# Recurrence scores: the second half's tokens kept in a turned order, and one product for two chunks at six levels

## The chip, the cores and the metric

The kernel runs on one core of one Trainium2 chip. A core has five engines that work side by side and are kept in step by semaphores: TensorE (PE in the profile; its weight loads are shown apart as PEld), VectorE (DVE), ScalarE (ACT), GpSimd (POOL) and SyncE (SP), which mostly issues DMAs. The metric is the device time of one execution in microseconds. Before the change it is 1434.34 us, the median of three runs (1434.25 to 1435.36).

## The reference

The reference is one block of a streaming encoder on 1024 tokens of 1024 channels in float32: a normalisation, a stick-breaking attention and a gated linear recurrence (HGRN2) side by side, a merge with per-channel gates, an output projection, an MLP with squared ReLU, and a last normalisation. The change is in the recurrence. For each of four heads with 128 channels:

```python
f = lb + (1.0 - lb) * sigmoid(f_raw);  k = (1.0 - lb) * sigmoid(-f_raw);  q = silu(q_hg)
# S_t = diag(f_t) S_{t-1} + k_t v_t^T,   o_t = S_t^T q_t, done by chunks:
bcum  = cumsum(log f)                                    # inside a chunk
decay = exp(bcum[t] - bcum[s])  where t >= s, else 0     # (t, s, d)
scores = einsum('td,sd,tsd->ts', q, k, decay)
o      = scores @ v + (q * exp(bcum)) @ state
state  = exp(b_last)[:, None] * state + (k * exp(b_last - bcum)).T @ v
```

The decay between a key's token s and a query's token t is a product over the tokens between them, one for each channel, so the scores of a chunk are not one product of two matrices.

## The kernel before, in words

The kernel holds the recurrence's data with channels on partitions and the 1024 tokens along the free dimension: for each head three tiles of 128x1024, `pp` (the forget factors f, called `dec`), `k` and `q`. Chunks are 128 tokens, eight of them; chunks 0 to 3 are the first half, 4 to 7 the second. The tile `sc` (128x1024) holds the scores of a head, for each chunk 128 key places on partitions by 128 query places. The tile `v` holds the values with tokens on partitions.

`hg_levels(h)` (line 1027) builds `sc` by levels. At level l the chunk is cut into blocks of 2H tokens, H = 2^l; each block has a left half of H tokens (keys) and a right half (queries). At that point `k` in a left half has been multiplied by the decay up to the half's end, `q` in a right half by the decay from the half's start, so the scores between the two are a plain product. After it the left keys are multiplied by the whole decay of the right half and the right queries by that of the left (lines 1144 and 1145), and the two whole decays by each other (line 1146): that prepares the next level. What each level does to get its scores differs:

- The diagonal and level 0 (H = 1) need no product of matrices: `pairs_of` multiplies keys and queries on VectorE, splits the result in a high and a low part (`hi_lo`: a cast on ScalarE, line 156, and a subtraction on VectorE, line 161), and `sums_of` adds over the channels with two products against a matrix of ones, 512 columns each, of the reduced float32 type that TensorE reads in one go.
- Level 1 (H = 2) does the same with two sets of pairs: four such products.
- Levels 2, 3, 4: `scores_of` (line 1034) makes one 128x128 float32 product per chunk, all keys by all queries, and line 1163 copies what a mask selects into `sc`, one copy on VectorE for each half.
- Levels 5 and 6 (H = 32, 64): 16 products of 32 columns from keys and queries that ScalarE had kept aside (line 1120), and eight of 64 columns; ScalarE then copies them to their partitions in `sc` (line 1170).

`hg_tail(h)` (line 1173) turns the keys onto partitions (`pk`), makes the state products with the values (`pkv`), adds up the states, makes the outputs (`pho`), normalises them and turns them back (`pot`) into `on`.

What sets the order of the work: the program is traced in the order of the code, and a planner places each instruction on its engine by priority and by its own forecast of durations; every engine then works in the order thus fixed, a DMA's issue included. PE's work is in two lanes, `main` (attention, recurrence) and `fill` (long projections). Inside a lane the order is kept; `open_block` lets the fill run at most two main blocks ahead of the last finished one (AHEAD = 2). The main program (lines 2370 to 2387) takes a level of head h and a step of head h-1's tail in turn, and after each advances the fill by a few steps of six 512-column products (FILL). The value projection `i_job` (line 948) is such a fill: for each block of 128 tokens, 24 products into `pji`, then ScalarE copies each head's 128 columns into that head's value tile (line 958). Head 0's tail waits with the state products until this job is done (`st.finish(j_i)`, line 1188).

Tiles of 4 KB a partition come from a pool of 40 (`slot`), those of 2 KB from a pool of ten (`slot_n`), PSUM banks from a pool of eight. A tile's place comes free when its last reader is done.

Of the kernel before, what the change touches and what calls it, by code (L numbers as in the profile page):

```python
# [19 lines left out]
P = 128  # L20
T = 1024
# [18 lines left out]
def kernel(  # L40
# [127 lines left out]
    def mul(out, a, b):  # L168
        return nc.vector.tensor_tensor(out=out, in0=a, in1=b, op=ALU.mult)  # L169

# [747 lines left out]
    def f_epilogue(h):  # L918
        def ep(ps, half):
            pp, k = hg_slot(h, "pp", half), hg_slot(h, "k", half)  # L920
            nc.scalar.activation(k, ps, AF.Sigmoid, scale=-1.0)
            nc.scalar.activation(pp, ps, AF.Sigmoid)
# [21 lines left out]

    u_i = wide_unit("wi", W_IN, C_I, HGW)
    u_i.__class__ = ByParts

    def i_job():
        unit = u_i

        vs = []

        def ep(ps, tb):
            for h in range(NHG):
                if tb == 0:
                    vs.append(slot(f"v{h}"))
                    hg[h, "v"] = vs[h]
                nc.scalar.copy(vs[h][:, tb * P : (tb + 1) * P], ps[:, h * P : (h + 1) * P])
            if tb == NT - 1:
                vs.clear()  # L960

        return st.add([unit], lambda: token_steps("pji", unit, xn, range(NT), ep, n=HGW))

    def silu_epilogue(h, key):
        def ep(ps, half):
            t = hg_slot(h, key, half)
            nc.scalar.activation(t, ps, AF.Sigmoid)
            if h < 2:
                x = slot_n(f"qx{h}_{half}", 512)
                nc.scalar.copy(x, ps)  # L970
                ps = x
            mul(t, ps, t)

        return ep
# [17 lines left out]
    def make_masks():  # L992
        mscr = slot_n("mscr", 4 * P, I32)
        mask_bits = hpool.tile([P, 4 * 512], U8, tag="h", name="masks")
        m_x, m_s, m_gt, m_odd = (mscr[:, i * P : (i + 1) * P] for i in range(4))
# [3 lines left out]
        after(nc.vector.tensor_scalar(out=m_odd, in0=m_s, scalar1=1, scalar2=None, op0=ALU.bitwise_and), bounded[0])  # L999
        nc.vector.tensor_tensor(out=m_x, in0=m_x, in1=m_s, op=ALU.bitwise_xor)  # L1000

        def add_mask(l, m_if):
# [3 lines left out]
            m = mask_bits[:, len(masks) * P : (len(masks) + 1) * P]  # L1006
            made = nc.vector.scalar_tensor_tensor(
                out=m, in0=m_s, scalar=1.0, in1=m_if, op0=ALU.is_equal, op1=ALU.mult
            )
            masks.append(m)  # L1010
            masked[0] = made

        for l in (0, *range(2, 5)):
            add_mask(l, m_gt)

        mul(m_odd, m_odd, m_gt)
        add_mask(1, m_odd)
        nc.vector.tensor_tensor(out=m_odd, in0=m_gt, in1=m_odd, op=ALU.subtract)
        add_mask(1, m_odd)
# [7 lines left out]
    def hg_levels(h):  # L1027
# [6 lines left out]
        def scores_of(name):  # L1034
            open_block("main")
            banks = []
            for half in range(2):
                S = bank(f"{name}_{half}")
                for c in range(4):
                    cs = slice((4 * half + c) * P, (4 * half + c + 1) * P)  # L1040
                    matmul(S[:, c * P : (c + 1) * P], k[:, cs], q[:, cs], start=True, stop=True)
                banks.append(S)
            return banks

        def pairs_of(name, *products):

            his, los = [], []
            for i, (a, b, w) in enumerate(products):
# [3 lines left out]
                x = mul(t.rearrange("p (n c) -> p n c", c=w) if w else t, a, b)  # L1052
# [28 lines left out]

        def diagonal(sums, behind=None):
# [3 lines left out]
        pairs = pairs_of(f"sd{h}", *((k[:, cs], q[:, cs], 0) for _, cs in halves()))  # L1086
# [7 lines left out]
        for l in range(7):  # L1094
            H = 1 << l
            n = T // (2 * H)
            if l <= 2:
                sums = sums_of(pairs)
            if l == 0:
                pairs = pairs_of(  # L1100
                    f"sl{h}_{l}", (blocks_of(k, 1)[:, :, 0, 0], blocks_of(q, 1)[:, :, 1, 0], 0)
# [3 lines left out]
            elif l == 1:  # L1105
                if h == 0:
                    u_i.split(3)
                kv, qv = blocks_of(k, 2)[:, :, 0], blocks_of(q, 2)[:, :, 1]
                pairs = pairs_of(
                    f"sl{h}_{l}",  # L1110
                    *((kv[:, :, i : i + 1].to_broadcast([P, T // 4, 2]), qv, 2) for i in (1, 0)),
                )
                if h == 0:
                    u_i.split(4)
            elif l < 5:
                banks = scores_of(f"sl{h}_{l}")
            elif l == 5:
                kept = tuple(slot_n(f"{n}k{h}", 512) for n in "kq")
                for i, (to, src) in enumerate(zip(kept, (k, q))):
                    nc.scalar.copy(  # L1120
                        to.rearrange("p (n h) -> p n h", h=H), blocks_of(src, H)[:, :, i, :]
                    )
# [1367 lines left out]
```

## Time and profile before

| | |
|---|---|
| median of three runs | 1434.34 us |
| profiled execution, its own time | 1434.48 us |
| its span, first to last instruction | 1432.7 us |
| granted TensorE clock, mean | 0.998 |
| TensorE busy | 1421.8 us, 99% of the span |
| VectorE busy | 1106.8 us, 77% |
| ScalarE busy | 678.9 us, 47% |
| GpSimd busy | 150.5 us, 11% |
| DMA, mean rate | 164 GB/s, 235.64 MB moved |

The recurrence runs from about 325 to 570 us of the span, between attention and the merge. How to read the rows: an engine, the line of the kernel, the operation, the tile written, an arrow and the tiles read, with buffer numbers left out (`sl` for the score banks of all heads and levels, `pji` for all value blocks). A float32 product of TensorE leaves two records for each instruction, one of the reduced type leaves one. Starts of PE records show its pace; their lengths overlap, since products are pipelined. Of a DMA, the time to landing is counted from its issue.

### The profile page before, as it was taken

What the parts mean: (1) busy time and instruction counts of PE and PEld (TensorE: products, weight loads), DVE (VectorE), ACT (ScalarE), POOL (GpSimd) and SP (SyncE); (2) the same over time, 40 slices, a digit from 0 to 9 for tenths busy, and PEclk for the clock granted to TensorE, in tenths of its full rate; (3) what the DMA queues carried; (4) which work ended last, traced back from release to release, by engine and by line L of the source; (5) the groups of instructions that cost most, each with busy time, mean ns of one, the idle gap of its engine ahead of it and who ended that gap; (6) DMA issues with size and microseconds to landing.
All of it is one profiled execution on the core that took longest, in us unless ns stands there. A gap on an engine that the chain in (4) does not pass through costs nothing.

```text
span 1432.7 us, 19220 instructions
## 1 busy us (share of the span) xinstructions
PE 1421.8 (99%) x7056; PEld 1195.2 (83%) x7056; DVE 1106.8 (77%) x1511; ACT 678.9 (47%) x1185; POOL 150.5 (11%) x340
## 2 busy tenths in 40 slices
PE   9999999999999999999999999999999999999998
PEld 8888888888888888888888888888888888888886
DVE  7579889888678898898797898666666758668765
ACT  6366676763233445333344673544444433524343
POOL 3012223210011031000000300000000000000042
PEclk9999999999999999999999999999999999999999
DMA  7024546435025775555476405444446974776825
GB/s 241 25 67 126 116 95 111 85 81 148 0 56 158 231 196 189 157 172 190 131 284 237 177 30 198 150 135 146 150 162 218 345 268 154 263 275 252 279 101 180
DMA packets 162038, 235.64 MB, mean 164 GB/s; under 512 B 26220, under 2 KB 93336, under 8 KB 161944
## 3 DMA queue, kind: packets, MB, share of 16 engines
q1 hardware_dynamic: 145480, 190.37, 39.9%
q0 software_dynamic: 11584, 34.61, 9.8%
q10 hardware_dynamic: 4880, 9.44, 1.9%
q8 instruction: 55, 0.90, 0.3%
q14 instruction: 39, 0.32, 0.1%
HBM read 167.27 MB, written 65.01 MB: 162 GB/s over the span
## 4 chain that ended last, share of the span: by engine, by line
PE 97%; DVE 1%; DMA 1%; ACT 1%; POOL 0%; issue 0%; SPq 0%; ACTq 0%; DVEq 0%
PE pm L128 21%; PE pX L128 9%; PE pW L128 6%; PE pY L128 6%; PE pjqk L128 5%; PE pga L128 4%; PE gX L128 4%; PE gY L128 4%; PE pjf L128 3%; PE pys L128 3%; PE pjq L128 3%; PE pji L128 3%; PE pyh L128 3%; PE pjv L128 3%; PE po L128 3%; PE sl L128 3%
## 5 line engine op out<-in xcount | busy, mean ns | idle before, releaser
L156 ACT CAST whid<-w 128x1024 fp32r<-128x1024 f32 x30 | 31.6, 1054 | 154.5 <-PE pm L128 89.8
L814 DVE TENSOR_TENSOR_SCAN rm<-rm,bits 128x511 f32<-128x511 f32 (+7 forms) x72 | 87.2, 1218 | 18.0 <-ACT rm L792 18.0
L128 PE MATMUL pm<-wlod,sh 128*128 128x512 f32 x240 | 93.5, 390 | 0.0
L128 PE MATMUL pm<-whid,sh 128*128 128x512 f32 x240 | 93.4, 389 | 0.0
L128 PE MATMUL pm<-whid,sl 128*128 128x512 f32 x240 | 93.4, 389 | 0.0
L128 PE MATMUL pm<-tl,sh 128*128 128x512 f32 (+1 forms) x210 | 81.3, 387 | 0.0
L128 PE MATMUL pm<-th,sl 128*128 128x512 f32 (+1 forms) x210 | 81.3, 387 | 0.0
L128 PE MATMUL pm<-th,sh 128*128 128x512 f32 (+1 forms) x210 | 81.3, 387 | 0.0
L161 DVE TENSOR_TENSOR wlod<-w,whid 128x1024 fp32r<-128x1024 f32 x30 | 36.6, 1222 | 53.9 <-ACT whid L156 53.9
L161 DVE TENSOR_TENSOR sl<-sa,sh 128x1024 fp32r<-128x1024 f32 x56 | 68.2, 1218 | 0.3 <-ACT sh L156 0.3
L2124 POOL TENSOR_SCALAR fss<-fss 128x1 f32<-128x1 f32 x8 | 4.5, 560 | 562.0 <-ACT fsc L2119 561.4
L156 ACT CAST wTh<-pw 128x512 fp32r<-128x512 f32 (+2 forms) x96 | 43.9, 487 | 40.9 <-PE pw L131 38.6
L156 ACT CAST sh<-sa 128x1024 fp32r<-128x1024 f32 x56 | 57.2, 1045 | 7.1 <-DMA sa<-ad 7.1
L128 PEld LDWEIGHTS pm<-wlod,sh 128*128 128x128 f32 x240 | 45.1, 188 | 9.7 <-DVE wlod L161 0.4
L128 PEld LDWEIGHTS pm<-whid,sh 128*128 128x128 f32 x240 | 45.1, 188 | 9.5
L128 PEld LDWEIGHTS pm<-whid,sl 128*128 128x128 f32 x240 | 45.0, 188 | 9.2
L161 DVE TENSOR_TENSOR wTl<-pw,wTh 128x512 fp32r<-128x512 f32 (+2 forms) x96 | 49.9, 546 | 3.4 <-ACT wTh L156 3.4
L169 DVE TENSOR_TENSOR bt<-bt,rm 128x511 f32<-128x511 f32 (+7 forms) x72 | 49.0, 685 | 4.4 <-DVE rm L814 0.5
L792 ACT ACTIVATE rm<-z 128x511 f32<-128x511 f32 (+4 forms) x96 | 48.2, 502 | 7.5 <-DMA osb<-osb 2.9
L128 PE MATMUL pX<-sql,t1h 128*128 128x512 f32 x128 | 49.9, 390 | 0.0
L128 PE MATMUL pX<-sqh,t1l 128*128 128x512 f32 x128 | 49.9, 390 | 0.0
L128 PE MATMUL pX<-sqh,t1h 128*128 128x512 f32 x128 | 49.8, 389 | 0.0
(936 smaller groups left out, 4479.3 us busy)
## 6 DMA issues: line engine op xcount, KB each, us to landing
w<-in_w_ff_dram SPq DMA_DIRECT2D x72, 512.0 KB, 6.0
sa<-ad SPq DMA_DIRECT2D x56, 512.0 KB, 7.0
ad<-a SPq DMA_DIRECT2D x32, 256.0 KB, 2.5
ad<-s SPq DMA_DIRECT2D x16, 512.0 KB, 5.5
tw<-in_w_out_dram POOLq DMA_DIRECT2D x24, 256.0 KB, 4.9
pr<-pd SPq DMA_DIRECT2D x10, 512.0 KB, 5.2
x<-in_x_dram SPq DMA_DIRECT2D x8, 512.0 KB, 10.0
xnl<-xnh POOLq DMA_DIRECT2D x8, 512.0 KB, 9.0
```

The lines of the kernel that those rows point to most:

```text
L128: return pe(nc.tensor.matmul(*a, **k))
L156: hi_last[0] = after(in_turn("act", nc.scalar.copy(dst, src)), hi_behind[0])
L161: nc.vector.tensor_tensor(out=dst, in0=src, in1=hi.bitcast(F32), op=ALU.subtract),
L169: return nc.vector.tensor_tensor(out=out, in0=a, in1=b, op=ALU.mult)
L792: nc.scalar.activation(rm[:, s0 + c0 - 1 : s0 + m - 1], z[:, c0:m], AF.Sigmoid, scale=-0.125)
L814: sc = nc.vector.tensor_tensor_scan(out=rr, data0=rr, data1=bits[:, 1024 - nk + a : 1024 - nk + b][:, ::-1], initial=rm[:, b : b + 1] if i ...
L2124: nc.gpsimd.tensor_scalar(out=ssq, in0=ssq, scalar1=1.0 / D, scalar2=EPS, op0=ALU.mult, op1=ALU.add)
```

## The change

The tokens of the second half are kept in another order: inside each block of 32 tokens the 16 pairs stand in reverse, so the place of a token has four bits (those of 2, 4, 8 and 16) flipped and the lowest one kept. At levels 1 to 4 the keys of the second half then stand in right halves and its queries in left halves, the other way round than in the first half. One product now takes chunk c of the first half and chunk c + 4 of the second together: 64 keys and 64 queries from each. For that the keys of both are put into one tile by a copy on ScalarE, where each key's column is also its place in the chunk, and the queries are read where they are, by an access pattern that steps from one half to the other. The two quadrants of the result that belong to one chunk are laid into `sc`; the two that cross chunks are not used. Levels 5 and 6, whose bits are not flipped, are done the same way, with the second half's scores copied across partitions by ScalarE. Level 1 no longer goes through pairs and sums.

The order is brought in where the data arise: the activations and multiplies that write `pp`, `k` and `q` of the second half read PSUM with groups of two backwards, and the tail's last activation turns `on` back. The values, which have tokens on partitions, are turned by a trip through DRAM: two blocks of tokens at a time are stored, and loaded back with rows in the new order, both on ScalarE's DMA queue. For this the value tiles hold two token blocks of all four heads each, where they held one head's eight blocks, and the copy out of PSUM is one for all heads. There are two masks for each level from 1 to 4.

```diff
@@ -167,6 +167,18 @@
 
     def mul(out, a, b):
         return nc.vector.tensor_tensor(out=out, in0=a, in1=b, op=ALU.mult)
+
+    def in_groups(t):
+        return t.rearrange("p (c g r) -> p c g r", g=16, r=2)
+
+    def turned_groups(t):
+        return in_groups(t)[:, :, ::-1, :]
+
+    def of_half(t, half):
+        return turned_groups(t) if half else t
+
+    def as_half(t, half):
+        return in_groups(t) if half else t
...
@@ -918,8 +930,9 @@
     def f_epilogue(h):
         def ep(ps, half):
             pp, k = hg_slot(h, "pp", half), hg_slot(h, "k", half)
-            nc.scalar.activation(k, ps, AF.Sigmoid, scale=-1.0)
-            nc.scalar.activation(pp, ps, AF.Sigmoid)
+            ps = of_half(ps, half)
+            nc.scalar.activation(as_half(k, half), ps, AF.Sigmoid, scale=-1.0)
+            nc.scalar.activation(as_half(pp, half), ps, AF.Sigmoid)
...
@@ -942,31 +955,40 @@
+    val_t, stored = [], []
     u_i = wide_unit("wi", W_IN, C_I, HGW)
     u_i.__class__ = ByParts
 
+    def turn_values():
+        while stored:
+            t, vd = stored.pop()
+            rows = vd.rearrange("(n g r) c -> n g r c", g=16, r=2)[:, ::-1]
+            for r in range(2):
+                nc.scalar.dma_start(t[r::2], rows[:, :, r])
+
     def i_job():
         unit = u_i
 
-        vs = []
-
         def ep(ps, tb):
-            for h in range(NHG):
-                if tb == 0:
-                    vs.append(slot(f"v{h}"))
-                    hg[h, "v"] = vs[h]
-                nc.scalar.copy(vs[h][:, tb * P : (tb + 1) * P], ps[:, h * P : (h + 1) * P])
-            if tb == NT - 1:
-                vs.clear()
+            if tb % 2 == 0:
+                val_t.append(slot(f"v{tb // 2}"))
+            cs = slice(tb % 2 * 512, (tb % 2 + 1) * 512)
+            turn_values()
+            nc.scalar.copy(val_t[-1][:, cs], ps)
+            if tb >= NT // 2 and tb % 2:
+                vd = dram(f"vd{tb}", [P, 1024])
+                nc.scalar.dma_start(vd, val_t[-1])
+                stored.append((val_t[-1], vd))
 
     def silu_epilogue(h, key):
         def ep(ps, half):
             t = hg_slot(h, key, half)
+            ps, t = of_half(ps, half), as_half(t, half)
             nc.scalar.activation(t, ps, AF.Sigmoid)
             if h < 2:
-                x = slot_n(f"qx{h}_{half}", 512)
+                x = as_half(slot_n(f"qx{h}_{half}", 512), half)
                 nc.scalar.copy(x, ps)
                 ps = x
             mul(t, ps, t)
@@ -992,31 +1014,26 @@
...
+            for op in ops or (ALU.mult,):
+                m = mask_bits[:, len(masks) * P : (len(masks) + 1) * P]
+                masked[0] = nc.vector.scalar_tensor_tensor(
+                    out=m, in0=m_s, scalar=1.0, in1=m_if, op0=ALU.is_equal, op1=op
+                )
+                masks.append(m)
+
+        add_mask(0, m_gt)
+        for l in range(1, 5):
+            add_mask(l, m_gt, ALU.mult, ALU.is_gt)
 
@@ -1031,25 +1048,41 @@
         dec, k, q = (hg[h, n] for n in ("pp", "k", "q"))
...
-        def scores_of(name):
+        def crossed(t, side, H, c=None, last=False):
+            n = (512 if c is None else P) // (2 * H)
+            step = 512 if H > 16 else 512 - H if side else 512 + H
+            at = t.offset + (c or 0) * P + (side * H + H - 1 if last else side * H)
+            return bass.AP(
+                tensor=t.tensor,
+                offset=at,
+                ap=[list(t.ap[0]), [step, 2], [2 * H, n], [0 if last else 1, H]],
+            )
+
+        def scores_of(name, H):
+            keys = slot_n(f"k{name}", 512)
+            nc.scalar.copy(
+                keys.rearrange("p (n s h) -> p s n h", s=2, h=H), crossed(k, 0, H)
+            )
             open_block("main")
-            banks = []
-            for half in range(2):
-                S = bank(f"{name}_{half}")
-                for c in range(4):
-                    cs = slice((4 * half + c) * P, (4 * half + c + 1) * P)
-                    matmul(S[:, c * P : (c + 1) * P], k[:, cs], q[:, cs], start=True, stop=True)
-                banks.append(S)
-            return banks
+            S = bank(name)
+            for c in range(4):
+                matmul(
+                    S[:, c * P : (c + 1) * P].rearrange("p (s n h) -> p s n h", s=2, h=H),
+                    keys[:, c * P : (c + 1) * P],
+                    crossed(q, 1, H, c),
+                    start=True,
+                    stop=True,
+                )
+            return S
 
...
@@ -1079,11 +1112,29 @@
                 right, m, S.rearrange("p (c n h) -> p c n h", c=NT, h=H)
             )
 
+        def lay_half(l, S, half):
+            H = 1 << l
+            side = 1 if l > 4 else 1 - half
+            to = sc[:, half * 512 : (half + 1) * 512].rearrange(
+                "p (c n two h) -> p c n two h", c=4, two=2, h=H
+            )[:, :, :, side]
+            src = S.rearrange("p (c s n h) -> p c s n h", c=4, s=2, h=H)[:, :, half]
+            if l < 5:
+                m = blocks_of(masks[2 * l - 1 + half], H)[:, :, side]
+                m = m.unsqueeze(1).to_broadcast([P, 4, P // (2 * H), H])
+                nc.vector.copy_predicated(to, m, src)
+                return
+            for b in range(P // (2 * H)):
+                r = 2 * b * H
+                nc.scalar.copy(
+                    to[r : r + H, :, b], src[r + half * H : r + (half + 1) * H, :, b]
+                )
+
...
@@ -1094,84 +1145,50 @@
         for l in range(7):
             H = 1 << l
             n = T // (2 * H)
-            if l <= 2:
+            if l < 2:
                 sums = sums_of(pairs)
             if l == 0:
                 pairs = pairs_of(
-                    f"sl{h}_{l}", (blocks_of(k, 1)[:, :, 0, 0], blocks_of(q, 1)[:, :, 1, 0], 0)
+                    f"sl{h}_{l}", (blocks_of(k, 1)[:, :, 0, 0], blocks_of(q, 1)[:, :, 1, 0])
                 )
                 if h == 0:
                     u_i.split(2)
-            elif l == 1:
-                if h == 0:
+            else:
+                S = scores_of(f"sl{h}_{l}", H)
+                if h == 0 and l == 1:
                     u_i.split(3)
-                kv, qv = blocks_of(k, 2)[:, :, 0], blocks_of(q, 2)[:, :, 1]
-                pairs = pairs_of(
-                    f"sl{h}_{l}",
-                    *((kv[:, :, i : i + 1].to_broadcast([P, T // 4, 2]), qv, 2) for i in (1, 0)),
-                )
-                if h == 0:
                     u_i.split(4)
-            elif l < 5:
-                banks = scores_of(f"sl{h}_{l}")
-            elif l == 5:
-                kept = tuple(slot_n(f"{n}k{h}", 512) for n in "kq")
-                for i, (to, src) in enumerate(zip(kept, (k, q))):
-                    nc.scalar.copy(
-                        to.rearrange("p (n h) -> p n h", h=H), blocks_of(src, H)[:, :, i, :]
-                    )
-            else:
-                open_block("main")
-                small_S = bank(f"sl{h}_5")
-                for i in range(2 * n):
-                    cs = slice(i * H // 2, (i + 1) * H // 2)
-                    matmul(
-                        small_S[0 : H // 2, cs], kept[0][:, cs], kept[1][:, cs],
-                        start=True, stop=True,
-                    )
-                S = bank(f"sl{h}_{l}")
-                for i in range(n):
-                    s0 = i * 2 * H
-                    matmul(
-                        S[0:H, i * H : (i + 1) * H],
-                        k[:, s0 : s0 + H],
-                        q[:, s0 + H : s0 + 2 * H],
-                        start=True,
-                        stop=True,
-                    )
             kv, qv, dv = (blocks_of(t, H) for t in (k, q, dec))
             left, right = (dv[:, :, i, H - 1 : H] for i in range(2))
-            mul(kv[:, :, 0, :], kv[:, :, 0, :], right.to_broadcast([P, n, H]))
-            mul(qv[:, :, 1, :], qv[:, :, 1, :], left.to_broadcast([P, n, H]))
+            if l == 0 or l > 4:
+                mul(kv[:, :, 0, :], kv[:, :, 0, :], right.to_broadcast([P, n, H]))
+                mul(qv[:, :, 1, :], qv[:, :, 1, :], left.to_broadcast([P, n, H]))
+            else:
+                for i, t in enumerate((k, q)):
+                    part = crossed(t, i, H)
+                    mul(part, part, crossed(dec, 1 - i, H, last=True))
             hg_level[0] = mul(right, right, left)
             if l == 0:
                 if h > 0:
                     diagonal(sums)
                 else:
                     first_sums = sums
-            elif l == 1:
-                if h == 0:
-                    diagonal(first_sums, pairs[3])
-                after(lay(masks[0], sums[0], 1), pairs[4] if h == 0 else None)
-            elif l == 2:
-                for m, S in zip(masks[-2:], sums):
-                    lay(m, S, 2)
-            if l < 2:
-                pass
-            elif l < 5:
-                for half_, cs in halves():
-                    nc.vector.copy_predicated(
-                        chunks(sc[:, cs]), over_chunks(masks[l - 1]), chunks(banks[half_])
-                    )
-            elif l == 6:
-                for G, src in ((H // 2, small_S), (H, S)):
-                    for i, b in enumerate(range(0, P, 2 * G)):
-                        part = src[0:G].rearrange("p (c b t) -> p c b t", c=NT, t=G)[:, :, i, :]
-                        nc.scalar.copy(chunks(sc)[b : b + G, :, b + G : b + 2 * G], part)
+            else:
+                if l == 1:
+                    if h == 0:
+                        diagonal(first_sums)
+                    lay(masks[0], sums[0], 1)
+                for half, _ in halves():
+                    lay_half(l, S, half)
             yield
 
     def hg_tail(h):
-        dec, k, q, v, sc = (hg.pop((h, n)) for n in ("pp", "k", "q", "v", "sc"))
+        dec, k, q, sc = (hg.pop((h, n)) for n in ("pp", "k", "q", "sc"))
+
+        def v(c):
+            at = c % 2 * 512 + h * P
+            return val_t[c // 2][:, at : at + P]
+
         on_t = slot(f"on{h}")
         fc = small.tile([P, NT], F32, tag="fc", name=f"fc{h}")
         nc.vector.tensor_copy(fc, chunks(dec)[:, :, P - 1])
@@ -1186,13 +1203,14 @@
             nc.scalar.copy(ktk[:, half * 512 : half * 512 + n * P], pk[:, : n * P])
         yield
         st.finish(j_i)
+        turn_values()
         open_block("main")
         for half in range(2):
             pkv = bank(f"pkv{h}_{half}")
             for j in range(4 - half):
                 c = 4 * half + j
                 cs, js = slice(c * P, (c + 1) * P), slice(j * P, (j + 1) * P)
-                matmul(pkv[:, js], ktk[:, cs], v[:, cs], start=True, stop=True)
+                matmul(pkv[:, js], ktk[:, cs], v(c), start=True, stop=True)
             for j in range(4 - half):
                 c = 4 * half + j
                 cs, js = slice(c * P, (c + 1) * P), slice(j * P, (j + 1) * P)
@@ -1218,7 +1236,7 @@
             for j in range(4):
                 c = 4 * half + j
                 cs, js = slice(c * P, (c + 1) * P), slice(j * P, (j + 1) * P)
-                matmul(po[:, js], sc[:, cs], v[:, cs], start=True, stop=c == 0)
+                matmul(po[:, js], sc[:, cs], v(c), start=True, stop=c == 0)
                 if c:
                     matmul(po[:, js], qh[:, cs], Ss[:, cs], start=False, stop=True)
             for j in range(4):
@@ -1235,7 +1253,8 @@
                 js = slice(j * P, (j + 1) * P)
                 transpose(pot[:, js], ons[half][:, js])
             nc.scalar.activation(
-                on_t[:, cs], pot, AF.Copy, scale=prm[:, HGN + h : HGN + h + 1]
+                as_half(on_t[:, cs], half), of_half(pot, half), AF.Copy,
+                scale=prm[:, HGN + h : HGN + h + 1],
             )
             yield
         ohg[h] = on_t
```

More of the change, by code (lines that the diff above doesn't have):

```diff
@@ L994, in make_masks @@
         mask_bits = hpool.tile([P, 4 * 512], U8, tag="h", name="masks")
-        m_x, m_s, m_gt, m_odd = (mscr[:, i * P : (i + 1) * P] for i in range(4))
+        m_x, m_s, m_gt = (mscr[:, i * P : (i + 1) * P] for i in range(3))
         nc.gpsimd.iota(m_x, pattern=[[1, P]], base=0, channel_multiplier=0)
@@ L998, in make_masks, with add_mask @@
         after(nc.vector.tensor_tensor(out=m_gt, in0=m_x, in1=m_s, op=ALU.is_gt), bounded[0])
-        after(nc.vector.tensor_scalar(out=m_odd, in0=m_s, scalar1=1, scalar2=None, op0=ALU.bitwise_and), bounded[0])
         nc.vector.tensor_tensor(out=m_x, in0=m_x, in1=m_s, op=ALU.bitwise_xor)
-        def add_mask(l, m_if):
+        def add_mask(l, m_if, *ops):
             nc.vector.tensor_scalar(
@@ L1051, in pairs_of @@
                 )
-                x = mul(t.rearrange("p (n c) -> p n c", c=w) if w else t, a, b)
+                x = mul(t, a, b)
                 after(x, turn_lo[0] if "sd0" in name else None)
@@ L1084, in diagonal @@
                 after(mul(chunks(sc[:, cs]), chunks(sums[i]), over_chunks(ident)), behind)
-        pairs = pairs_of(f"sd{h}", *((k[:, cs], q[:, cs], 0) for _, cs in halves()))
+        pairs = pairs_of(f"sd{h}", *((k[:, cs], q[:, cs]) for _, cs in halves()))
         for _, cs in halves():
```

14 lines of the change are left out of this document (1 added, 13 removed).

## The prediction

> **What bounds the kernel now.** I read the page first, then stretches, then TensorE's waits.
>
> ```profile
> span 1432.7 us, 19220 instructions
> PE 1421.8 (99%) x7056; PEld 1195.2 (83%) x7056; DVE 1106.8 (77%) x1511; ACT 678.9 (47%) x1185; POOL 150.5 (11%) x340
> PE 97%; DVE 1%; DMA 1%; ACT 1%; POOL 0%; issue 0%; SPq 0%; ACTq 0%; DVEq 0%
> ```
> ```profile
> 325.00:580.00 255.00, 255.00 (x1490) 217.54 (x1489) 206.61 (x316) 100.28 (x225) 31.66 (x40) 1.00 0.48 139
> 400.00:410.00 10.00, 10.00 (x60) 8.76 (x59) 5.47 (x15) 3.63 (x16) 0.00 (x0) 1.00 0.00 0
> ```
> ```profile
> PE warm L128 <- POOL ident masks.py:199: 2.2, 1, 2.2
> PE po L128 <- DVE wTl L161: 1.1, 2, 0.8
> ```
>
> The first fence is from the page (busy time, and the chain that ended last by engine), the second from the table of stretches, the third from the waits of TensorE. PE carries 97% of the ending chain and is busy 1421.8 of 1432.7 us. The changed code runs in the stretch 325 to 580 us; PE is busy there for all 255.00 us, VectorE for 206.61, ScalarE for 100.28. TensorE's longest wait is at the start (2.2 us); later only 1.1 us in two places before `po`. So a microsecond of PE work removed here is one gained, if nothing comes late in its place. The work around the recurrence is a fill of long products that the planner lays between the short main blocks.
>
> **PE work: the levels.** The timeline of PE for head 1 (start, length, group):
>
> ```profile
> 386.83 0.39 PE L128 MATMUL sl<-sl_h,ones 128*128 128x512 f32 x1
> ...
> 389.44 0.48 PE L128 MATMUL pji<-wih,xnh 128*128 128x512 f32 x1
> ...
> 392.03 0.39 PE L128 MATMUL pji<-wih,xnl 128*128 128x512 f32 x1
> 392.36 2.02 PE L128 MATMUL sl<-q,k 128*128 128x128 f32 x16
> 394.13 0.48 PE L128 MATMUL pji<-wih,xnh 128*128 128x512 f32 x1
> 394.45 0.40 PE L128 MATMUL pji<-wil,xnh 128*128 128x512 f32 x1
> 394.68 0.40 PE L128 MATMUL pji<-wih,xnl 128*128 128x512 f32 x1
> ...
> 396.99 1.95 PE L128 MATMUL sl<-q,k 128*128 128x128 f32 x16
> 398.69 0.48 PE L128 MATMUL pji<-wih,xnh 128*128 128x512 f32 x1
> ...
> 411.63 1.20 PE L128 MATMUL sl<-qk,kk 128*32 128x32 f32 x32
> ...
> 413.83 0.50 PE L128 MATMUL pjf<-xnh,wf3h 128*128 128x512 f32 x1
> ```
>
> From the start of a block to the next projection product: levels 1 and 2 together 389.44 - 386.83 = 2.61 us, level 3 1.77, level 4 1.70, levels 5 and 6 together 2.20: 8.28 a head, 33.1 for four. A full float32 block of eight 128x128 products (16 records, two passes each) takes 1.70, so one product 0.2125. Afterwards every level from 1 to 6 has four such products, 0.85; six levels make 5.1 a head, 20.4 in all. That is 12.7 less. Of it 3 x 0.85 a head are levels 2 to 4, cut from eight products to four; level 1 loses 0.91 (four 512-column products) and gets 0.85; levels 5 and 6 go from 2.20 to 1.70.
>
> A block also has edges. The projection product after one needs 0.32 to the next (394.13 to 394.45), where the usual step is 0.23 (394.45 to 394.68), and 0 to 0.1 is lost ahead (392.03 to 392.36 against 0.23). I take 0.15 a block. Levels 1/2, 3, 4, 5/6 make four blocks now, six afterwards: two more in each of four heads, 8 x 0.15 = 1.2. PE nets **-11.5**.
>
> What no row shows is a moving operand read in pieces: the queries of a level come as runs of 2 to 64 floats from two places 512 columns apart. All moving operands of the rows above are contiguous. Bounds: no cost, as for a VectorE multiply of level 0, which takes the same 0.68 on every second element (`sl_x` below) as `sl_l` takes on a contiguous tile; or double, as for the copy under a mask below, 1307 ns through gapped places against 730 in whole chunks. I take none: a float32 product draws 128 columns in 0.2125 us, where the 512-column ones draw 512 in 0.23, so it asks for data at about a quarter of a rate that PE is seen to get. [...]
>
> **VectorE and ScalarE.** One tile or line each, ns min/median/max:
>
> ```profile
> L1163 DVE COPY_PREDICATED sc<-masks,sl x24: 709/730/737, 351.5 to 531.8; 128x512 f32<-128x512 uint8 x24
> L1078 DVE COPY_PREDICATED sc<-masks,sl x12: 1296/1307/1316, 344.3 to 515.9; 128x512 f32<-128x512 uint8 x12
> L169 DVE TENSOR_TENSOR sl_x<-k,q x12: 682/684/693, 332.5 to 504.1; 128x512 f32<-128x512 f32 x12
> L161 DVE TENSOR_TENSOR sl_l<-sl_x,sl_h x12: 667/683/687, 334.9 to 505.5; 128x512 fp32r<-128x512 f32 x12
> L156 ACT CAST sl_h<-sl_x x12: 619/622/628, 333.8 to 504.8; 128x512 fp32r<-128x512 f32 x12
> L1120 ACT COPY kk<-k x4: 617/621/624, 357.3 to 532.6; 128x512 f32<-128x512 f32 x4
> L1170 ACT COPY sc<-sl x12: 356/361/580, 367.2 to 541.7; 32x256 f32<-32x256 f32 x8, 64x512 f32<-64x512 f32 x4
> ```
>
> VectorE loses per head two multiplies (0.68) and two subtractions (0.68) of level 1, two gapped masked copies of level 1 (1.31) and six of whole chunks (0.73): 9.7 us. It gains eight masked copies of 256 elements. By halves of the two rows each is 0.37 to 0.65, so 2.9 to 5.2. VectorE gets 4.5 to 6.8 a head lighter. The level multiplies keep their count and size. The masks are one small operation fewer in front, nothing.
>
> ScalarE loses two casts (0.62), two copies of kept halves (0.62) and three copies into the scores (1.3): 3.8. It gains six key copies (0.62 each by the same row), four copies of 32 partitions (at most 0.36) and two of 64 (at most 0.58): 6.3. That is +2.5 a head, or 10 us on an engine that has 155 free here; the 32 value copies become eight, a little less. Hidden. If the cover went, what showed would be the key copy on the path: multiply, key copy, products, multiply. Its tightest place is level 4 of head 0:
>
> ```profile
> 353.31 0.68 DVE L169 TENSOR_TENSOR q<-q,pp 128x512 f32<-128x512 f32 x1
> 354.59 1.61 PE L128 MATMUL sl<-q,k 128*128 128x128 f32 x13
> ```
>
> The query multiply ends at 353.99, the products start at 354.59, so 0.6 us is left. The key copy starts after the key multiply, 0.6 earlier than the query multiply ends, and runs beside it: it costs about 0.1 of that. VectorE, which is late there, is also lighter. I take 0.
>
> The half turned round costs no instruction: the same activations and multiplies read PSUM or the tile in groups of two, backwards. They lie on engines with room: 0.
>
> **The values: a new trip through DRAM.** The values of the second half must stand in the new order of partitions. Two 512 KB stores and four 256 KB loads go on ScalarE's queue, each pair of loads behind its store's landing. The pair of blocks 4 and 5 has a whole block of projection (24 products, 5.5 us, and main blocks between) to land. The pair 6 and 7 has not: its store is issued at the end of the projection, and head 0's tail then needs block 6 in the seventh state product.
>
> ```profile
> 399.92 0.39 PE L128 MATMUL pji<-wih,xnl 128*128 128x512 f32 x1
> 400.15 1.72 PE L128 MATMUL pkv<-v,pp 128*128 128x128 f32 x14
> 401.63 0.48 PE L128 MATMUL pjf<-xnh,wf3h 128*128 128x512 f32 x1
> ...
> 407.20 0.60 PE L128 MATMUL pho<-v,sc 128*128 128x128 f32 x4
> ```
> ```profile
> 400.83 0.76 ACT L958 COPY v<-pji 128x128 f32<-128x128 f32 x4
> ...
> 407.40 0.60 ACT L921 ACTIVATE k<-pjf 128x512 f32<-128x512 f32 x1 [5.82 <-PE pjf L128]
> ```
> ```profile
> L1186 ACT COPY pp<-pk x8: 486/544/593, 377.1 to 546.8; 128x512 f32<-128x512 f32 x4, 128x384 f32<-128x384 f32 x4
> ```
> ```profile
> L1378 ACTq DMA_DIRECT2D pd<-p x10: 321/326/357, 115.0 to 517.7; - x10
> ```
> ```profile
> hd<-h POOLq DMA_DIRECT2D x8, 512.0 KB, 3.4
> wo02r<-in_w_o_sb_dram SPq DMA_DIRECT2D x1, 512.0 KB, 3.8
> ad<-s SPq DMA_DIRECT2D x16, 512.0 KB, 5.5
> w<-in_w_ff_dram SPq DMA_DIRECT2D x72, 512.0 KB, 6.0
> ```
>
> These are PE around the last value projection, ScalarE at that point, a PSUM copy of 128x512, an issue on ScalarE's queue, and issues with their median time to landing. From the projection's last start (399.92, a step 0.23): copy 0.59, store 3.4 (as `hd`, since DMA is 0.00 busy from 400 to 410 us), second issue 0.33, loads 3.8 (as `wo02r`): 8.1 us. PE has six state products (6/7 of 1.48, 1.27) and, if the planner puts them ahead, the 24 projection products up to 407.20 (5.57): 6.8. The fill may run two main blocks ahead and no further, so that is all. The wait is then 1.3 us. With the medians of loaded stretches (5.5 and 6.0) it is 0.59 + 5.5 + 0.33 + 6.0 - 6.8 = 5.6; with all the fill behind the waiting product, 8.1 - 1.27 = 6.8; with more ahead, 0. I take **+2**, near the quiet rows. ScalarE stands in its queue for the store, about 3.4 us from 401; behind that are level 5's key copy, which PE could not use before the state products anyway, and the next epilogue at 407.40. Hidden. The loads of the earlier pair are issued a block later, 5.5 us against the store's 3.4, so ScalarE hardly stands for them. Heads 1 to 3 find all values landed.
>
> **Sum.** -12.7 + 1.2 + 2 = -9.5 against the profiled execution's 1434.48 (span 1432.7, 1.8 around it; the runs' median 1434.34 is 0.14 lower): **1425 us**.
>
> **Rivals.** The store and loads land slowly or the order is bad (5.6 to 6.8 us of wait): 1434.48 - 11.5 + 6.2 = 1429. For it: the two loaded rows above. Against: DMA is idle at that place. A wait of that length may do more: the granted clock is 1.00 in both stretches quoted, but the longest wait of PE in the whole run, 2.2 us, is too short to try it; were half of such a wait lost again to a slower clock, 1432. [...]
>
> The other side: the moving operand in pieces. If products of levels 1 to 4, runs of 2 to 16 floats, took double, 16 blocks would grow by 0.85: +13.6, 1439. It decides from 70% (9.5 of 13.6). For it speaks the masked copy's 1307 against 730, against it the multiply's equal 0.68.
>
> The third: the gain is given back behind the levels. The value tiles now hold all four heads each, so the first three heads' tails free none:
>
> ```profile
> L128 PE MATMUL pho<-v,sc x64: 270/275/275, 407.2 to 560.7; 128*128 128x128 f32 x64
> ```
>
> Their last use starts at 560.7 us, where the tiles of heads 0 to 2 were free from their own tails on. A pool of 40 tiles then has up to three fewer for loads and splits, and PE reaches each load sooner. One load that PE waits for in full (6.0) makes 1431, two 1437. Against: no PE wait for a DMA in this stretch now, and ScalarE and VectorE wait little there.
>
> **How the numbers follow.** The forecast has 0.62, with its own range 1422 (no wait for values, edges at half) to 1428. The slow trip has 0.15 (of it 0.05 with the slower clock), pieces 0.10, giving back 0.13, of which 0.05 ends near 1431, 0.05 within 1432 to 1437, 0.03 above. 0.2% is 2.9 us, about what a measurement of this kernel can tell from no change. Faster: 0.62 + 0.15 and a part of the 0.05, 0.80; same 0.07; slower 0.10 + 0.03 = 0.13. The range reaches to 1434, which leaves the pieces and the worse half of giving back outside.
>
> **What would show it.** Right: `sl` blocks of four products in 0.85 at levels 1 to 6 whatever their runs; masked copies of 256 elements at 0.37 to 0.65; PE waiting on the value loads, once, 1 to 3 us before `pkv` near 398; PE 100% busy elsewhere from 330 to 570. Wrong: a level's four products above 1.2; a PE wait above 4 there or a granted clock below 1.00 behind it; new waits of PE on DMA after 420.

## The result, and the profile after

The changed kernel takes 1429.01 us, median of six runs (1427.89 to 1429.33), against 1434.3 for the kernel before: a ratio of 0.996, with a 95% interval of 0.9948 to 0.9973. It is faster by about 5 us, where 9.5 were forecast. The profiled execution takes 1429.28 us.

From the page, busy time by engine and the chain that ended last by engine; then the stretch of the recurrence (PE, its weight loads, DVE, ACT, POOL busy; granted clock; DMA share; GB/s); then the waits of TensorE:

```profile
span 1427.5 us, 18779 instructions
PE 1411.4 (99%) x6848; PEld 1186.3 (83%) x6848; DVE 1087.4 (76%) x1494; ACT 684.2 (48%) x1181; POOL 146.6 (10%) x340
PE 96%; DMA 1%; DVE 1%; ACT 1%; POOL 0%; issue 0%; SPq 0%; ACTq 0%; DVEq 0%
```
```profile
325.00:580.00 255.00, 250.06 (x1304) 213.31 (x1303) 190.37 (x307) 106.69 (x224) 28.62 (x40) 0.99 0.51 150
```
```profile
PE pkv L128 <- DMA v<-vd: 4.9, 1, 4.9
PE warm L128 <- POOL ident masks.py:199: 2.2, 1, 2.2
PE po L128 <- DVE wTl L161: 0.7, 2, 0.4
```

VectorE is 19.4 us lighter than before (1106.8 to 1087.4), ScalarE 5.3 heavier. PE, busy in all of the 255 us before, now lacks 4.94 us of them, all in one wait: `pkv`, the state product, for the values that come back from DRAM. Before, PE's longest wait was 2.2 us, at the start. The clock in this stretch is 0.99, not 1.00.

The level blocks of head 1 on PE (start, length, group), which answer to the rows of head 1 before:

```profile
379.75 0.39 PE L128 MATMUL sl<-sl_h,ones 128*128 128x512 f32 x1
379.97 0.39 PE L128 MATMUL sl<-sl_l,ones 128*128 128x512 f32 x1
380.20 1.07 PE L128 MATMUL sl<-q,ksl 128*128 128x128 f32 x8
381.02 0.48 PE L128 MATMUL pji<-wih,xnh 128*128 128x512 f32 x1
...
383.88 1.05 PE L128 MATMUL sl<-q,ksl 128*128 128x128 f32 x8
384.68 0.48 PE L128 MATMUL pji<-wih,xnh 128*128 128x512 f32 x1
...
387.50 1.05 PE L128 MATMUL sl<-q,ksl 128*128 128x128 f32 x8
388.31 0.48 PE L128 MATMUL pji<-wih,xnh 128*128 128x512 f32 x1
```

From a block's start to the next group's start, level 1 takes 381.02 - 380.20 = 0.82, level 2 0.80 and level 3 0.81. The first two rows are level 0's sums, which now stand right ahead of level 1's block. Before, levels 1 and 2 took 2.61 together, level 3 1.77 and level 4 1.70.

By tile, ns min/median/max: the copies into the scores, and the key copies:

```profile
L1125 DVE COPY_PREDICATED sc<-masks,sl x32: 423/434/816, 343.2 to 525.7; 128x256 f32<-128x256 uint8 x32
L1111 DVE COPY_PREDICATED sc<-masks,sl x4: 1307/1316/1319, 341.4 to 499.5; 128x512 f32<-128x512 uint8 x4
L1063 ACT COPY ksl<-k x24: 609/622/708, 334.0 to 535.2; 128x512 f32<-128x512 f32 x24
```

The new masked copies take 0.434 us, the key copies 0.622.

Now the place that waits. First the chain that ended last between 390 and 412 us (start, length, step), then PE there, then stretches around it:

```profile
393.59 0.59 ACT v L977
...
394.21 2.60 DMA vd<-v
...
396.83 0.53 ACTq L967
...
397.41 7.84 DMA v<-vd
...
405.29 0.80 PE pkv L128 x2
```
```profile
399.96 0.39 PE L128 MATMUL pjf<-xnh,wf3l 128*128 128x512 f32 x1
405.29 0.80 PE L128 MATMUL pkv<-v,pp 128*128 128x128 f32 x2 [4.94 <-DMA v<-vd]
405.88 1.92 PE L128 MATMUL sl<-q,ksl 128*128 128x128 f32 x8
407.59 1.06 PE L128 MATMUL pho<-v,sc 128*128 128x128 f32 x4
...
411.42 0.40 PE L128 MATMUL pjf<-xnh,wf3l 128*128 128x512 f32 x1
411.66 0.39 PE L128 MATMUL pjf<-xnh,wf3h 128*128 128x512 f32 x1
```
```profile
394.00:396.00 2.00, 2.00 (x15) 1.79 (x14) 1.79 (x6) 0.18 (x1) 0.00 (x0) 1.00 0.50 201
402.00:404.00 2.00, 0.00 (x0) 0.00 (x0) 0.05 (x1) 0.00 (x0) 0.00 (x0) 1.00 0.25 102
406.00:410.00 4.00, 4.00 (x21) 4.00 (x21) 3.17 (x6) 1.02 (x4) 0.00 (x0) 0.50 0.00 0
```

The store of the last pair of blocks takes 2.60 us, the loads behind it 7.84. The share of 0.50 in the store's stretch is a mean: nothing moves in its first microsecond, and in its second the engines are busy to 0.99 and move 401 GB/s. Between 402 and 404 us, with nothing but the loads under way, the share is a quarter, 102 GB/s, as 4 of 16 engines working without a break would give. PE is through with its fill 4.94 us before `pkv` can start. Then it runs at half clock: a level block that takes 0.81 elsewhere takes 407.59 - 405.88 = 1.71, and the granted clock is 0.50 from 406 to 410 us. Narrower stretches give the ends of that:

```profile
404.40:404.60 0.20, 0.00 (x0) 0.00 (x0) 0.00 (x0) 0.00 (x0) 0.00 (x0) 0.91 0.16 61
404.60:404.80 0.20, 0.00 (x0) 0.00 (x0) 0.00 (x0) 0.00 (x0) 0.00 (x0) 0.50 0.01 0
...
411.20:411.40 0.20, 0.20 (x2) 0.14 (x1) 0.00 (x0) 0.20 (x3) 0.00 (x0) 0.52 0.00 0
411.40:411.60 0.20, 0.20 (x2) 0.18 (x1) 0.00 (x0) 0.20 (x4) 0.00 (x0) 1.00 0.00 0
```

The clock falls at about 404.56 (1.00 up to there and 0.50 behind it make the mean of 0.91 in that fifth of a microsecond) and is back at 411.39. Of this PE worked from 405.29 on, 6.1 us at half speed, which is 3.05 us lost.

### The profile page after: what moved, and what is told of

The parts are those of the page before. It is cut to its first block, busy times and chain, and to the rows that moved or that the text cites. A ratio compares the mean times of both kernels' runs of the same rounds, so it can differ in the third digit from the quotient of the medians.

```text
span 1427.5 us, 18779 instructions
## 1 busy us (share of the span) xinstructions
PE 1411.4 (99%) x6848; PEld 1186.3 (83%) x6848; DVE 1087.4 (76%) x1494; ACT 684.2 (48%) x1181; POOL 146.6 (10%) x340
## 4 chain that ended last, share of the span: by engine, by line
PE 96%; DMA 1%; DVE 1%; ACT 1%; POOL 0%; issue 0%; SPq 0%; ACTq 0%; DVEq 0%
PE pm L128 21%; PE pX L128 9%; PE pW L128 6%; PE pY L128 6%; PE pjqk L128 5%; PE pga L128 4%; PE gX L128 4%; PE gY L128 4%; PE pjq L128 3%; PE pys L128 3%; PE pji L128 3%; PE pyh L128 3%; PE pjv L128 3%; PE pjf L128 3%; PE po L128 3%; PE z L128 2%
```

## Experiments

Each is the changed kernel with one edit, or, where it says so, the kernel of the first experiment with one edit. The theory: the levels' saving is there in full, and one wait of 4.9 us and the half clock behind it took most of it away. The rivals: a trip through DRAM is slow as such; the clock has nothing to do with it; or the gain is missing somewhere else.

**The second half projected first.**

```diff
-        return st.add([unit], lambda: token_steps("pji", unit, xn, range(NT), ep, n=HGW))
+        return st.add([unit], lambda: token_steps("pji", unit, xn, (4, 5, 6, 7, 0, 1, 2, 3), ep, n=HGW))
```

(and `val_t` becomes a dictionary by pair of blocks.)

> The value projection takes the token blocks in the order 4 5 6 7 0 1 2 3, so that both trips through DRAM land under the projection of the first half; nothing else is changed. Theory (the trip's wait of 4.9 us and the half clock behind it, about 3.0 us, ate the gain): no wait of TensorE before pkv, clock 1.00 from 400 to 412 us, 1429.0 - 4.9 - 3.0 = 1421.1. Rival one (the wait alone counts, the longer products behind it are no loss): 1424.1. Rival two (the missing gain lies behind the levels, in late loads or tiles that come free late): the wait goes, but as much comes back as a new wait, 1426 to 1429.

Measured: 1421.33 us (1421.05 to 1421.87), 0.9911 of before (0.9894 to 0.9927). From its page and its stretches:

```profile
PE 1408.4 (99%) x6848; PEld 1183.2 (83%) x6848; DVE 1087.3 (77%) x1494; ACT 684.2 (48%) x1181; POOL 147.7 (10%) x340
325.00:580.00 255.00, 255.00 (x1339) 217.23 (x1338) 193.93 (x311) 110.36 (x229) 29.61 (x41) 1.00 0.53 158
```

PE is busy for all 255.00 us again, the clock is 1.00, and PE waits for no value any more. It is the theory's number within 0.3. This kernel is the fastest of those that compute the whole; the order of a loop was worth 7.7 us. PE's busy time is 1408.4 against 1411.4 in the changed kernel, though the products are the same: the 3.0 between is the half clock.

**The rows unturned.**

```diff
-            rows = vd.rearrange("(n g r) c -> n g r c", g=16, r=2)[:, ::-1]
             for r in range(2):
-                nc.scalar.dma_start(t[r::2], rows[:, :, r])
+                nc.scalar.dma_start(t[r::2], vd[r::2])
```

> Store and loads are as in the changed kernel, same bytes and same place in ScalarE's queue, but the loads read every second row of the block in rising order, so that the slowest dimension of the DRAM side counts 64 and not 4. The turning of the values is left out, so the second half's values stand in the wrong order. Theory (the loads took 8 us because only 4 of the 16 DMA engines had packets): the loads land in 2 to 4 us from issue, TensorE waits 0 to 1 us, 1421 to 1422. Rival (a load right behind a store of the same bytes is slow as such, whatever its pattern): loads still about 8 us, wait 4.9, 1429.

Measured: 1422.37 us (1421.67 to 1422.47). Its chain at the same place, its PE at the end of the wait, and a stretch with its loads alone:

```profile
394.28 2.62 DMA vd<-v
...
397.42 3.47 DMA v<-vd
```
```profile
400.93 0.49 PE L128 MATMUL pkv<-v,pp 128*128 128x128 f32 x2 [0.52 <-DMA v<-vd]
```
```profile
399.00:400.00 1.00, 1.00 (x6) 0.84 (x5) 0.00 (x0) 0.00 (x0) 0.00 (x0) 1.00 0.79 270
```

The loads, same bytes, behind the same store, land in 3.47 us where the turned ones took 7.84 (counted from the issue of the second of the two); PE waits 0.52 us. So the store ahead is not the cause: the pattern of the loads is. The edit changes two things in it, the count of its outermost dimension (the turned rows are read as 4 blocks by 16 pairs, the unturned ones as 64 rows) and the falling order of the rows. With the turned loads alone under way the DMA share is 0.25, at 102 GB/s, and in the trace of the changed kernel 4 of their packets are under way at most times, each of 4 KB and a median of 0.159 us; with the unturned loads alone the share is 0.79, at 270 GB/s. That the 4 blocks and the 4 packets under way belong together is my reading; which of the two things makes the loads slow was not shown, for falling rows with a larger count were not run.

**PE kept busy in the wait, and the wait cut short.** Three kernels, with 50, 10 and 5 products of the identity:

```diff
+                if h == 0 and c == 6:
+                    spare = bank("spare")
+                    for _ in range(50):
+                        matmul(spare[:, 0:P], ident, ident, start=True, stop=True)
                 matmul(pkv[:, js], ktk[:, cs], v(c), start=True, stop=True)
```

> Fifty 128x128 float32 products of the identity (10.65 us by 0.213 each) stand in front of head 0's seventh state product, the one that waits for the values; their results are not used. The 24 fill products (5.5 us) that stood there then come behind it. TensorE does not pause. Theory (the half clock from 405 to 411 us comes from the pause of 4.9 us and costs 3.0): granted clock 1.00 throughout, 1429.0 + 5.5 - 3.0 = 1431.5. Rival (the clock or the product lengths there have another cause, or cost nothing): 1434.5.

> The changed kernel with ten products of the identity (2.2 us by 0.223 each) ahead of the waiting state product, their results unused; the 24 fill products stay ahead of it, so the pause shrinks from 4.9 to about 2.7 us. Theory: work and pause give 1421.3 + 2.2 + 2.7 = 1426.2. If the clock falls after any pause of this size: up to 2.8 more, 1429.0, and a granted clock of 0.5 behind it; if only a longer pause brings it, 1426.2 and 1.00 throughout.

> The same with five products (1.1 us), so a pause of about 3.8 us. Work and pause give 1421.3 + 1.1 + 3.8 = 1426.2. With the loss behind the pause of 4.9 us (2.8): 1429.0, granted clock 0.5 for about 6 us; with none, 1426.2 and 1.00. Together with the run of ten products it brackets the pause from which the clock falls.

PE at the wait in the kernels with 50, 10 and 5, and stretches of each behind it:

```profile
394.49 11.33 PE L128 MATMUL spare<-ident 128*128 128x128 f32 x100
405.65 0.39 PE L128 MATMUL pkv<-v,pp 128*128 128x128 f32 x2
```
```profile
406.00:410.00 4.00, 4.00 (x23) 3.40 (x22) 1.31 (x4) 0.26 (x1) 0.00 (x0) 1.00 0.00 0
```
```profile
405.69 0.49 PE L128 MATMUL pkv<-v,pp 128*128 128x128 f32 x2 [2.75 <-DMA v<-vd]
```
```profile
406.00:408.00 2.00, 2.00 (x20) 2.00 (x19) 1.79 (x6) 0.86 (x4) 0.00 (x0) 1.00 0.03 8
```
```profile
405.15 0.79 PE L128 MATMUL pkv<-v,pp 128*128 128x128 f32 x2 [3.57 <-DMA v<-vd]
```
```profile
404.60:404.80 0.20, 0.00 (x0) 0.00 (x0) 0.00 (x0) 0.00 (x0) 0.00 (x0) 0.68 0.00 0
...
407.80:408.00 0.20, 0.20 (x3) 0.20 (x2) 0.20 (x1) 0.19 (x2) 0.00 (x0) 0.50 0.00 0
408.00:408.20 0.20, 0.20 (x4) 0.20 (x2) 0.20 (x1) 0.20 (x1) 0.00 (x0) 0.79 0.00 0
```

| added products | added work, us | pause of PE, us | clock behind it | PE busy above 1408.4 and the added work | time, us |
|---|---|---|---|---|---|
| none | 0 | 4.94 | 0.50 until 411.39 | 3.0 | 1429.01 |
| 5 | 1.1 | 3.57 | 0.50 until 408.08 | 1.4 | 1428.11 |
| 10 | 2.2 | 2.75 | 1.00 | 0.1 | 1426.48 |
| 50 | 11.2 | 0 | 1.00 | 0.5 | 1432.46 |

The times are medians; pause, clock and busy time are from the one profiled execution of each kernel. The fifth column is from the pages: PE is busy 1411.4, 1410.9, 1410.7 and 1420.1 us. With the first experiment's 1421.33 as the floor, floor + added work + pause + fifth column gives 1429.3, 1427.4, 1426.4 and 1433.0, so these four terms make up each time within 0.7. Fifty products took 405.65 - 394.49 = 11.16 us, not the 10.65 written, which is a part of that run's 1.0 above the theory; had the 3.0 another cause than the pause, that run would have come to 1421.3 + 11.2 + 3.0 = 1435.5. The pause makes the clock fall: in the profiled executions one of 2.75 us did not, one of 3.57 us did. With five products neither of the two prices written down came, but one between them: half the loss (1.4), and a half clock of 3.4 us where about 6 were expected.

How far this bracket holds for other executions is open. The four runs of the kernel with ten products reach from 1425.97 to 1428.41, and the mean clock on record is 0.998 for the slowest and 0.999 for the other three, so the clock may have fallen in that one too; it has no profile.

**No trip.**

```diff
-                vd = dram(f"vd{tb}", [P, 1024])
-                nc.scalar.dma_start(vd, val_t[-1])
-                stored.append((val_t[-1], vd))
+                pass
```

> No store and no loads of values: the tiles are used as they leave PSUM. The turning of the values is left out, so the second half's values stand in the wrong order. It is what the change would be with a free trip. Theory: 1421.1, within 1 us of the run that projects the second half first, since a hidden trip costs nothing. Rival (the trip costs ScalarE's queue or the DMA engines something even when hidden): this one is faster than that run by over 1 us.

Measured: 1421.21 us (1420.85 to 1421.53), 0.1 from the first experiment, inside both their ranges. A trip that lands in time is free here, and there is nothing more to be had from the values.

**The levels' products twice** (edit on the kernel of the first experiment):

```diff
-            for c in range(4):
+            for c in (0, 1, 2, 3, 0, 1, 2, 3):
                 matmul(
                     S[:, c * P : (c + 1) * P].rearrange("p (s n h) -> p s n h", s=2, h=H),
```

> On top of the kernel that projects the second half first (1421.3), each level's four products are made twice, the second time over the same result. 24 blocks by 0.81 us (the step of such a block in the changed kernel) are 19.4 us more PE work. Theory (PE alone sets the pace between 325 and 580 us, so a product there is worth its whole length): 1421.3 + 19.4 = 1440.7. Rival (a part of a level's time is the chain of copies and multiplies on ScalarE and VectorE, beside which the products are free): less than 1435.

Measured: 1443.03 us (1442.9 to 1443.55), 21.7 more. From its page, and a block of head 1:

```profile
PE 1429.8 (99%) x7040; PEld 1204.8 (84%) x7040; DVE 1087.6 (75%) x1494; ACT 684.1 (47%) x1181; POOL 146.5 (10%) x340
```
```profile
385.73 1.98 PE L128 MATMUL sl<-q,ksl 128*128 128x128 f32 x16
387.46 0.48 PE L128 MATMUL pji<-wih,xnh 128*128 128x512 f32 x1
```

PE is busy 21.4 us longer, and the time grows by as much: work of PE in the level blocks is worth its whole length, and the chains of copies beside it set next to nothing (one wait of 0.2 us on a key copy). The size was off by 2.3, because four more products behind four others take longer than the first four. The block shown is level 1's and takes 387.46 - 385.73 = 1.73; level 2's of the same head takes 392.01 - 390.31 = 1.70, so its second four take 1.70 - 0.81 = 0.89. That is also the mean over all blocks (21.4 / 24), and 24 x 0.08 = 1.9.

**Queries that lie side by side** (on the kernel of the first experiment):

```diff
-                    crossed(q, 1, H, c),
+                    q[:, c * P : (c + 1) * P].rearrange("p (s n h) -> p s n h", s=2, h=H),
```

> On top of the kernel that projects the second half first (1421.3), each product reads 128 queries that lie side by side instead of runs of 2 to 64 from two places. The second half's queries are left out, so the scores are not the reference's. Theory (a moving operand in pieces costs nothing): 1421.3 within 0.6, blocks at 0.81 as before. Rival (pieces cost something that the step of 0.81 hides, 0.85 for four contiguous products having been an overestimate): faster by 24 times the difference, 1419 for 0.1 us a block.

Measured: 1421.03 us (1420.66 to 1421.21), 0.3 below the first experiment. Level 1 of head 1:

```profile
379.79 1.05 PE L128 MATMUL sl<-q,ksl 128*128 128x128 f32 x8
380.59 0.48 PE L128 MATMUL pji<-wih,xnh 128*128 128x512 f32 x1
```

The step is 0.80 with contiguous queries, 0.82 with runs of two. Reading the moving operand in pieces costs at most 0.02 us a block.

## Why the prediction was right, and which of its terms were not

The forecast was 1425, faster. It came out faster at 1429.01, 4 us later: 1 us outside the range that the prediction gives the forecast itself (1422 to 1428) and inside the wider one that reaches to 1434. The saving on PE came by the mechanism forecast. The value trip did not come as forecast, and two signs that the prediction names for being wrong were there: a wait of PE above 4 us at `pkv`, and a clock below 1.00 behind it. Two terms erred against the forecast and one for it. That they partly cancel is luck: with the saving as forecast, the same wait and clock would have made 1434.48 - 11.5 + 4.9 + 3.0 = 1431.

| term | forecast, us | measured, us | from |
|---|---|---|---|
| PE's work in the levels, with edges | -11.5 | -13.4 | PE busy 1421.8 before, 1408.4 in the first experiment |
| wait for the values | +2 | +4.9 | PE's waits |
| slower clock behind the wait | 0 | +3.0 | PE busy 1411.4 against 1408.4 |
| sum | -9.5 | -5.5 | profiled executions: 1429.28 - 1434.48 = -5.2 |

**PE's work.** The mechanism is as forecast, and its size was put too low by 1.9. A block of four products takes 0.81, not 0.85: the 0.2125 for one product came from blocks of eight, where the later ones take longer (0.89 for the last four, above). That is 24 x 0.04 = 1.0. The rest, 0.9, is left for the edges: 1.2 was forecast for eight more blocks, and -13.4 leaves about 0.3. The rows fit this. The step behind a block is 0.32 before and after, 0.09 above the usual 0.23 where the forecast took 0.15, so eight more blocks are 0.7; and the four blocks of levels 5 and 6 of before lost 0.09 ahead of them, 0.4 in all, which is gone.

**The moving operand in pieces** was taken at nothing, and is: in the changed kernel's profile 21 of the 24 blocks take 0.80 to 0.82, level 1 with its runs of two 0.82 in every head. Two take 0.91, level 4 of head 2 and level 6 of head 3, where the same levels of the other heads take 0.80 or 0.81; one, behind the wait, takes 1.71 at half clock. With contiguous queries levels 1 to 4 of head 1 take 0.80 to 0.81. That rival, 1439, falls.

**VectorE and ScalarE.** The masked copies of 256 elements take 0.434, between the 0.37 and 0.65 given; VectorE is 19.4 / 4 = 4.9 us a head lighter, as forecast (4.5 to 6.8). ScalarE's 5.3 in all instead of some 10 minus the value copies changes nothing. PE's waits of 0.2 us and more name no key copy.

**The value trip** is the step that failed, and in it the term "loads 3.8 (as `wo02r`)". The place, head 0's seventh state product, was right, and so was the cover: the last projection product ended near 393.5, and PE had work until 405.29 - 4.94 = 400.35, that is 6.9 us, against 6.8 in the forecast. The copy took 0.59 as written, the store 2.60 instead of 3.4. The loads took 0.53 + 7.84 instead of 0.33 + 3.8. The row of `wo02r` was of another pattern, and I compared only the bytes. The loads of this change read rows in four blocks, in falling order, and the diff shows it (`n g r c` with n = 4); this was a fact to be had before. With the loads at the 3.47 of the unturned rows, the wait was 0.52.

**The clock** stood only in a rival, at 0.05, where half of the wait was to be lost again. That half was my guess; no run shows it. For a wait of 4.9 it gives 2.5. Measured is 3.0, and the last section shows how the loss went with the pause. It belonged into every outcome with a wait as long as this.

**The third rival**, a gain given back behind the levels by tiles that come free late, did not come: behind 412 us PE waits for no DMA, and the first experiment gains 1434.48 - 1421.37 = 13.1 us between the profiled executions with the same tiles.

The rival of the slow trip was priced at 1429, and 1429 was measured, but not by its sum: it had 1.9 less saving and no clock. The measured wait of 4.9 and the measured saving, without the clock, would give 1434.48 - 13.4 + 4.9 = 1426.

## What to carry to other kernels

Price a DMA by a row of the same pattern, not of the same size: here the same bytes landed in 7.84 us with the rows turned and in 3.47 us unturned, with a DMA share of 0.25 and 0.79. Where PE is the bound, a pause costs its length, and a longer one (here 3.57 us, but not 2.75) costs again in the clock behind it, so a new wait of that size is worth moving, by issuing its DMA earlier, even at the price of another loop order. Before a trip through DRAM is put on the path, ask which of the work that needs no trip could come last.

## What the runs showed of the hardware

A pause of TensorE of 2.75 us left the granted clock at 1.00; one of 3.57 us brought 0.50 until 408.08 and one of 4.94 us 0.50 until 411.39. Both times the clock fell near 404.6, before the loads had landed: 404.67 - (405.15 - 3.57) = 3.1 us after the shorter pause began and 404.56 - (405.29 - 4.94) = 4.2 us after the longer. It stayed down for 408.08 - 404.67 = 3.4 and 411.39 - 404.56 = 6.8 us, the second time twice as long as the first; PE began again 0.5 us after the fall with the shorter pause and 0.7 us after it with the longer. The loss came in two sizes: 1.4 us with the 3.4 us of half clock, 3.0 with the 6.8. What sets the moment of the fall and its length was not shown. No pause between 2.75 and 3.57 us was tried, and whether the same pause costs the same in another execution is open: no run here was made to show it.

Four 128x128 float32 products took 0.81 us at the head of a block and 0.89 behind four others, the mean of 24 blocks (0.91 in the block of level 1 above), and fifty in a row 11.16 / 50 = 0.223 each: the price of a short block is not that of a long one divided.
